# Weight sums on VectorE, and product reads as ScalarE copies with accumulating DMAs, in a two-layer streaming encoder

## The chip, the cores and the metric

The kernel runs on one core of one Trainium2 chip. A core has five engines, each with its own queue of instructions in a fixed order: TensorE (PE, with its weight loads as PEld), VectorE (DVE), ScalarE (ACT), GpSimd (POOL) and SyncE (SP). SP here does nothing but issue DMAs; POOL and ACT issue some as well. Data wait in SBUF, matmuls write to banks of PSUM, and DRAM holds inputs, outputs and spilled intermediates. Engines wait for each other and for DMAs by semaphores. The metric is the time of one execution on the device in microseconds, as the median of several runs.

## The reference

One inference step of a hybrid encoder of two layers, `DEPTH = 2`, for 1024 prompt tokens and 8 x 16 sample tokens, so nine tiles of 128 tokens with `D_MODEL = 1024` and `D_FF = 4096`. Layer 0 has sliding-window attention with its own keys and values, layer 1 attends over shared keys and values. What the change touches is the end of each layer:

```python
def mlp(x, g_norm, w_up, w_down):
    return jnp.square(jax.nn.relu(rmsnorm(x, g_norm) @ w_up)) @ w_down
...
        hp = hp + mlp(hp, g_mlp[layer], w_up[layer], w_down[layer])
        hs = hs + mlp(hs, g_mlp[layer], w_up[layer], w_down[layer])
```

The product with `w_down` (4096 x 1024) is added to the residual `hp` or `hs`. After layer 0 the sum is what layer 1 reads, after layer 1 it is the output. All data are float32.

## The kernel before, in words

A layer runs four stages: `attention`, `wo_phase` (output projection and norm), `mlp_up` and `mlp_down`. The residual of tile t lies in DRAM as `xd[t]`, 128 x 1024. Every float32 operand of a matmul is split in two parts, a rounded one (`hi`, cast on ACT, L128) and the remainder (`lo`, subtracted on DVE, L134), and a product is formed by three matmuls (`mm3`, L746 to L748).

The down projection does not multiply the plain blocks. `mlp_up` writes 20 forms of the hidden activations per half of `D_FF` to DRAM (`hd`, stores from POOL, L911). For each half, `mlp_down` multiplies each form with a combination of the eight raw weight blocks of that half (`W_FORMS`). There are 40 such products a layer. Each is three banks (one for each of three token tiles) of 12 matmuls of 128x512. The result of a product is then added to or taken from some of six outputs (`OUT_FORMS`): three parts of three tiles each (`PARTS`), by two halves of 512 columns. The products are put in chains (`CHAINS`): in a chain the same three banks go on accumulating, and only the difference between the output rows of a product and the next has to be read. So a bank is read between two products, and the next product of the chain may write to it only after that. The list `seq` holds the products in order with their reads; there are 41 reads a layer, each of three banks. Six banks give two chains room.

For product n the stage does this:

- `load_w` (SP): raw weight blocks not yet held, 1 MB each, into `r0` to `r10`; issued three products ahead (`AHEAD`).
- `load_h` (SP): the form, 768 KB, into `a0`, `a1` or `a2` in turn; it waits until PE is through with the product that used that buffer. `load` also ties these loads to each other in order.
- `add_w` (L1067): the sum or difference of two weight blocks, 128x2048, into `s0` or `s1`, on POOL, two products ahead. A combination of one block needs none.
- `split_w`: the split of the weights into `w0` or `w1`, and of the form in place, on ACT and DVE, one product ahead.
- the matmuls, and behind each bank the reads (L1119): DVE adds the bank into the tile of the residual.

The residual tiles `x0` to `x8` are loaded into SBUF at the start of the stage (`load_x`, at products 0, 1 and 3 of the order `X_AT`) and held there; a tile is stored after its last read. `DOWN_HOME` places all buffers of the stage, in an order that decides which of them share space with the last buffers of `mlp_up`, so that a load into them waits for the stores of `hd` from that space.

The text of the program is not the order on the engines: a planner orders each queue by priorities and its own estimates. A wait stops every later instruction of the same queue. In layer 0 `prep_bias`, called at product 20, prepares biases of layer 1 with DMAs of its own on SP.

## Time and profile before

| | us |
|---|---|
| median of 3 runs | 2477.91 (2471.18 to 2479.93) |
| the profiled execution | 2474.45 |
| its span, first to last instruction | 2472.3 |
| first and last start of `mlp_down` matmuls, layer 0 | 803.6 to 1196.8 |
| the same, layer 1 | 2079.1 to 2467.5 |
| granted TensorE clock, mean | 0.980 of full speed |

A row of instructions in the profile names the line, the engine, the operation, and the tiles as out<-in with buffer numbers left out: `a<-hd` is the load of a form, `s<-r,r` a weight sum, `w<-s` a split of a weight sum, `x<-x,ps_c` a read of a bank into the residual. Behind the count stand the busy time in us and the mean of one in ns, then the idle time before it and whoever ended it. Where a row stands for one tile, the three numbers are the least, the middle and the greatest duration in ns. A table of stretches gives the busy time of the engines and the number of instructions, then the granted clock, the mean busy share of the 16 DMA engines, and the rate in GB/s. Times in an order of events are us from the start of the span. Busy shares are averages over stages with different limits, so the stage concerned is read by itself.

### The profile page before, as it was taken

How to read it: one execution, taken by the hardware profiler on the slowest of the kernel's cores; microseconds unless marked ns; L12 is line 12 of the kernel's file. 1: busy time of each engine (PE TensorE's matmuls, PEld its weight loads, DVE VectorE, ACT ScalarE, POOL GpSimd, SP SyncE). 2: the span in 40 equal slices, each digit the busy share in tenths (PEclk: the TensorE clock that was granted, in tenths of full speed). 3: DMA queues.
4: the chain of work that ended last, by engine and by line, in shares of the span. 5: the costliest groups of instructions: out<-in, count | busy, mean ns of one | idle time of the engine just before them, and what ended most of it. 6: DMA issues, size and time to landing. Idle time of an engine off the chain costs nothing.

```text
span 2472.3 us, 33316 instructions
## 1 busy us (share of the span) xinstructions
PE 2311.3 (93%) x11429; PEld 1911.4 (77%) x11429; DVE 1848.3 (75%) x3128; ACT 1273.0 (51%) x2503; POOL 914.6 (37%) x956
## 2 busy tenths in 40 slices
PE   8998999999999789989999999998999998899989
PEld 6787877888888667767778788786888887677767
DVE  6788787665665888999577867877656566798995
ACT  3777674655555333333277766655555554233332
POOL 4434334122322554553233434344222223444650
PEclk9999999999999999999999999998999999899999
DMA  7445554243434643525544655543334336524523
GB/s 249 126 116 162 167 175 166 92 146 116 163 131 178 250 150 105 197 79 195 167 144 133 189 163 169 181 157 129 125 119 149 131 130 225 187 94 141 175 74 130
DMA packets 216376, 375.38 MB, mean 152 GB/s; under 512 B 51144, under 2 KB 125840, under 8 KB 216208
## 3 DMA queue, kind: packets, MB, share of 16 engines
q1 hardware_dynamic: 193136, 300.89, 37.8%
q0 software_dynamic: 21776, 67.65, 7.5%
q10 hardware_dynamic: 1296, 4.72, 0.5%
q8 instruction: 90, 1.47, 0.3%
q14 instruction: 78, 0.64, 0.1%
HBM read 241.23 MB, written 130.90 MB: 151 GB/s over the span
## 4 chain that ended last, share of the span: by engine, by line
PE 62%; DVE 18%; DMA 9%; issue 6%; ACT 3%; POOL 1%; SPq 0%; DVEq 0%; ACTq 0%; POOLq 0%
DVE a L134 5%; PE ps_x L746 5%; PE ps_x L748 5%; PE ps_x L747 5%; DVE w L134 3%; DMA a<-hd 3%; DVE x L1119 3%; PE ps_mm L217 3%; PE ps_c L746 3%; PE ps_c L747 3%; PE ps_c L748 3%; PE ps_mm L219 3%; PE ps_mm L218 3%; PE ps_y L748 2%; PE ps_y L747 2%
## 5 line engine op out<-in xcount | busy, mean ns | idle before, releaser
L746 PE MATMUL ps_c<-w,a 128*128 128x512 f32 x960 | 386.3, 402 | 62.2 <-DVE x L1119 54.7
L747 PE MATMUL ps_c<-w,a 128*128 128x512 f32 x960 | 385.0, 401 | 24.0 <-DVE w L134 23.9
L1067 POOL TENSOR_TENSOR s<-r,r 128x2048 f32<-128x2048 f32 x56 | 291.2, 5202 | 281.2 <-DVE w L134 160.4
L748 PE MATMUL ps_c<-w,a 128*128 128x512 f32 x960 | 383.1, 399 | 5.4 <-DVE a L134 5.4
L911 POOL DMA_DIRECT2D hd<-h x272 | 147.9, 544 | 582.4 <-ACT h L820 280.0
L134 DVE TENSOR_TENSOR a<-a 128x1536 fp32r<-128x1536 f32 x80 | 258.5, 3232 | 46.4 <-ACT a L128 46.4
L746 PEld LDWEIGHTS ps_c<-w,a 128*128 128x128 f32 x960 | 185.9, 194 | 113.7 <-DVE x L1119 36.9
L747 PEld LDWEIGHTS ps_c<-w,a 128*128 128x128 f32 x960 | 185.9, 194 | 67.6 <-DVE w L134 29.4
L128 ACT CAST a<-a 128x1536 fp32r<-128x1536 f32 x80 | 118.5, 1481 | 213.9 <-DMA a<-hd 213.8
L748 PEld LDWEIGHTS ps_c<-w,a 128*128 128x128 f32 x960 | 186.0, 194 | 47.1 <-DVE a L134 8.0
L128 ACT CAST w<-s 128x2048 fp32r<-128x2048 f32 x56 | 107.1, 1912 | 212.0 <-PE ps_c L748 177.9
L134 DVE TENSOR_TENSOR w<-s,w 128x2048 fp32r<-128x2048 f32 x56 | 176.3, 3150 | 21.8 <-ACT w L128 21.7
L1119 DVE TENSOR_TENSOR x<-x,ps_c 128x512 f32<-128x512 f32 x246 | 158.8, 676 | 35.7 <-PE ps_c L748 35.5
L217 PE MATMUL ps_mm<-w,hh 128*128 128x512 f32 x432 | 172.9, 401 | 6.5 <-POOL w L185 2.1
L219 PE MATMUL ps_mm<-w,hl 128*128 128x512 f32 x432 | 171.9, 399 | 1.2 <-DMA hl<-hTd 1.0
L218 PE MATMUL ps_mm<-w,hh 128*128 128x512 f32 x432 | 170.9, 396 | 1.4 <-DVE w L190 1.1
L746 PE MATMUL ps_x<-sx,w 128*128 128x512 f32 (+1 forms) x408 | 158.9, 390 | 3.4 <-ACT h L867 2.5
L747 PE MATMUL ps_x<-sx,w 128*128 128x512 f32 (+1 forms) x408 | 155.2, 380 | 0.0
L748 PE MATMUL ps_x<-sx,w 128*128 128x512 f32 (+1 forms) x408 | 155.2, 380 | 0.0
L128 ACT CAST w<-ru 128x512 fp32r<-128x512 f32 (+1 forms) x160 | 110.0, 708 | 84.4 <-PE ps_y L747 32.0
L134 DVE TENSOR_TENSOR ptl<-ps_tr,pth 128x512 fp32r<-128x512 f32 x180 | 122.4, 685 | 23.5 <-ACT pth L128 18.0
L134 DVE TENSOR_TENSOR w<-ru,w 128x512 fp32r<-128x512 f32 (+1 forms) x160 | 126.6, 793 | 15.2 <-ACT w L128 15.1
(280 smaller groups left out, 5972.6 us busy)
## 6 DMA issues: line engine op xcount, KB each, us to landing
a<-hd SPq DMA_DIRECT2D x80, 768.0 KB, 4.2
hd<-h POOLq DMA_DIRECT2D x272, 192.0 KB, 2.5
ru<-in_w_up SPq DMA_DIRECT2D x64, 512.0 KB, 3.8
r<-in_w_down SPq DMA_DIRECT2D x32, 1024.0 KB, 8.7
x<-xd SPq DMA_DIRECT2D x41, 512.0 KB, 6.4
o<-oTd SPq DMA_DIRECT2D x52, 256.0 KB, 4.4
xd<-xo SPq DMA_DIRECT2D x18, 512.0 KB, 2.8
xo<-xd SPq DMA_DIRECT2D x18, 512.0 KB, 3.7
```

The costliest lines, as they stand in the source:

```text
L128: a = nc.scalar.copy(hi, src)
L134: return a, e.tensor_tensor(lo, src, hi.bitcast(F32), ALU.subtract)
L217: nc.tensor.matmul(ps, a, w[:, 0, k, :], start=(k == 0), stop=False)
L218: nc.tensor.matmul(ps, a, w[:, 1, k, :], start=False, stop=False)
L219: self.lp = nc.tensor.matmul(ps, b, w[:, 0, k, :], start=False, stop=(k == KC - 1))
L746: a = mm(ps, ah, bh, start=first, stop=False, skip_group_check=True)
L747: mm(ps, ah, bl, start=False, stop=False, skip_group_check=True)
L748: return a, mm(ps, al, bh, start=False, stop=last, skip_group_check=True)
L911: return lambda p, z: self.nc.gpsimd.dma_start(self.hd[c // 4][:, p, c % 4], z)
L1067: nc.gpsimd.tensor_tensor(src[n], x, y, ALU.add if plus else ALU.subtract)
L1119: tt(x, x, banks[i], ALU.add if v > 0 else ALU.subtract)
```

## The change

It has four parts, all in or for `mlp_down`.

- The weight sums are made by DVE instead of POOL.
- Of the 41 reads a layer, only the last read of each of the six outputs is still a DVE addition. For it, SP loads the three half tiles (128x512, 256 KB) of the residual from DRAM into `f` buffers (six, in turn) at that product, DVE adds the bank, and SP stores the half tile to its destination.
- The other 35 reads become ACT copies of the three banks into an `o` buffer (128 x 3 x 512; four, in turn), with the sign as the scale, and one accumulating DMA of the buffer into the residual in DRAM, issued by POOL.
- The `x` tiles and their loads at the start are gone. `o` and `f` buffers take their places in `DOWN_HOME`. In DRAM the residual is now three tensors `xp`, one for each part, and `xd[t]` is a view of one.

```diff
-                s=([P, 4, 512], F32), x=([P, D], F32),
+                s=([P, 4, 512], F32), o=([P, 3, 512], F32), f=([P, 512], F32),
...
-                nc.gpsimd.tensor_tensor(src[n], x, y, ALU.add if plus else ALU.subtract)
+                tt(src[n], x, y, ALU.add if plus else ALU.subtract)
...
-            def load_x(i):
-                for t in PARTS[i]:
-                    load(xs[t], self.xd[t])
...
                 a, w = aa.pop(n), ws.pop(n)
+                ends, adds = {}, {}
+                for o, v in reads:
+                    part, h = divmod(o, 2)
+                    if left[o] == n:
+                        for i in range(3):
+                            ends[o, i] = take(f"f{nf % 6}")
+                            nf += 1
+                            nc.sync.dma_start(ends[o, i], self.xd[PARTS[part][i]][:, N[h]])
+                    else:
+                        adds[o] = take(f"o{no % 4}")
+                        no += 1
                 for i in range(3):
...
                     for o, v in reads:
-                        x = xs[PARTS[o // 2][i]][:, N[o % 2]]
-                        tt(x, x, banks[i], ALU.add if v > 0 else ALU.subtract)
-                    for part in {o // 2 for o, _ in reads}:
-                        if last[part] == n:
-                            t = PARTS[part][i]
-                            nc.sync.dma_start(out(t), xs[t])
+                        part, h = divmod(o, 2)
+                        if o in adds:
+                            nc.scalar.activation(adds[o][:, i], banks[i], AF.Copy, scale=float(v))
+                        else:
+                            x, t = ends[o, i], PARTS[part][i]
+                            tt(x, x, banks[i], ALU.add if v > 0 else ALU.subtract)
+                            nc.sync.dma_start(out(t)[:, N[h]], x)
+                for o, z in adds.items():
+                    part, h = divmod(o, 2)
+                    dst = self.xp[part][:, :, N[h]].rearrange("t p n -> p t n")
+                    nc.gpsimd.dma_start(dst, z, accum_op=ALU.add)
...
-            self.xd = [dram([P, D], f"xd{t}") for t in range(NTILE)]
+            self.xp = [dram([3, P, D], f"xp{i}") for i in range(3)]
+            self.xd = {t: self.xp[i][n] for i in range(3) for n, t in enumerate(PARTS[i])}
...
 DOWN_HOME = (
-    "s0", "s1", "r0", "r1", "r2", "r3", "x5", "x6", "x7", "bias", "r4", "r5", "+384", "x2", "x3", "x0", "+640",
-    "a0", "x4", "x1", "x8", "r6", "a1", "a2", "w0", "w1", "r7", "r8", "r9", "r10",
+    "s0", "s1", "r0", "r1", "r2", "r3", "o2", "o3", "bias", "r4", "r5", "+384", "o0", "f0", "f1", "f2", "+640",
+    "a0", "f3", "f4", "o1", "f5", "r6", "a1", "a2", "w0", "w1", "r7", "r8", "r9", "r10",
 )
```

In the built program the other stages keep their order on every engine, apart from the first steps of layer 1's attention, which the planner weaves into the end of layer 0's `mlp_down` a little differently. POOL has only the 35 accumulating DMAs between the last store of `hd` and the next stage. An accumulating DMA waits for the copies it sends and for the accumulating DMA before it that went to the same output; an ACT copy waits for the accumulating DMA that last used its buffer.

More of the change, by code (lines that the diff above doesn't have):

```diff
@@ L978, in mlp_down @@
                 a=([P, 2, 4, 3 * P], F32R), w=([P, 2, 4, 512], F32R), r=([P, 4, 512], F32),
-                s=([P, 4, 512], F32), x=([P, D], F32),
+                s=([P, 4, 512], F32), o=([P, 3, 512], F32), f=([P, 512], F32),
             )
-            homes, slots, xs = {}, {}, {}
+            homes, slots = {}, {}
             def fresh(tag):
@@ L1000, in mlp_down @@
                         slots[t] = fresh(t)
-            for t in range(NTILE):
-                xs[t] = slots.pop(f"x{t}")
             N = [slice(0, 512), slice(512, 1024)]
@@ L1023, in mlp_down @@
                     left[i] = n
-            last = {i // 2: max(left[i], left[i ^ 1]) for i in left}
             aa, ws = {}, {}
@@ L1077, in mlp_down @@
             banks = None
+            nf = no = 0
             def early(n):
                 return self.tc.high_priority(EARLY[n]) if n < len(EARLY) else nullcontext()
-            def load_x(i):
-                for t in PARTS[i]:
-                    load(xs[t], self.xd[t])
             for n in range(AHEAD):
@@ L1089, in mlp_down @@
                     load_h(n)
-                if n in X_AT:
-                    load_x(X_AT[n])
             add_w(0)
@@ L1099, in mlp_down @@
                     load_w(n + AHEAD)
-                if n + AHEAD in X_AT:
-                    load_x(X_AT[n + AHEAD])
                 split_w(n + 1)
@@ L1782 @@
 AHEAD = 3
-X_AT = {0: 2, 1: 1, 3: 0}
 WO_ORDER = [[0, 4, 1, 5, 2, 6, 7, 3, ST], [0, 4, 1, 5, 6, 2, 7, 3, ST]]
```

## The prediction

> **What bounds the kernel now.** I read the page first, then the down-projection stage (`mlp_down`) by the stretches in which its products run, since the change touches only this stage and the first steps after it. Two rows of the page, and the product matmuls (`ps_c`) over four stretches (columns: stretch, its length, busy time and count of PE, PEld and DVE, granted clock, DMA share, GB/s):

> ```profile
> span 2472.3 us, 33316 instructions
> PE 2311.3 (93%) x11429; PEld 1911.4 (77%) x11429; DVE 1848.3 (75%) x3128; ACT 1273.0 (51%) x2503; POOL 914.6 (37%) x956
> ...
> 803.00:900.00 97.00, 77.83 (x315) 61.70 (x316) 19.41 (x30) 0.93 0.67 233
> 900.00:1197.00 297.00, 266.06 (x1127) 213.21 (x1125) 59.35 (x92) 0.98 0.40 136
> 2079.00:2180.00 101.00, 81.03 (x313) 64.22 (x314) 19.95 (x31) 0.86 0.51 184
> 2180.00:2468.00 288.00, 265.71 (x1129) 214.42 (x1127) 58.73 (x92) 0.98 0.36 123
> ```

> PE is 93% busy over the span, but not here. A stretch in which it never waits gives its pace; a stretch of the up-projection beside it shows that PE can hold that pace at full clock:

> ```profile
> 980.00:1020.00 40.00, 40.00 (x178) 33.14 (x177) 34.60 (x26) 16.82 (x10) 13.00 (x4) 1.00 0.57 197
> 1920.00:1960.00 40.00, 40.00 (x201) 34.01 (x200) 24.76 (x40) 21.84 (x37) 10.84 (x20) 1.00 0.40 137
> ```

> 178 matmuls in 40 us are 0.225 us each; a product is 36, so 8.1 us, and a layer's 1440 are 324 us. Layer 0 takes 97 + 297 = 394 us and layer 1 101 + 288 = 389: 70 and 65 us lost. At 0.225 us the counts split that into a start (97 - 315 x 0.225 = 26 us; 31 us) and the rest (44; 35). The waits of PE in each layer's stage (total us, times, longest) name who is late most, and the order of time shows why (a step of DVE, POOL and ACT from layer 1):

> ```profile
> PE ps_c L746 <- DVE x L1119: 29.8, 13, 6.0
> PE ps_c L746 <- DVE x L1119: 24.9, 12, 5.9
> ```

> ```profile
> 2193.79 1.27 DVE L1119 TENSOR_TENSOR x<-x,ps_c 128x512 f32<-128x512 f32 x2
> 2194.99 2.28 DVE L134 TENSOR_TENSOR w<-s,w 128x2048 fp32r<-128x2048 f32 x1
> 2197.19 0.67 DVE L1119 TENSOR_TENSOR x<-x,ps_c 128x512 f32<-128x512 f32 x1
> 2197.79 5.79 DVE L134 TENSOR_TENSOR a<-a 128x1536 fp32r<-128x1536 f32 x1
> ...
> 2197.34 4.62 POOL L1067 TENSOR_TENSOR s<-r,r 128x2048 f32<-128x2048 f32 x1 [5.09 <-DVE w L134]
> ...
> 2200.34 1.91 ACT L128 CAST w<-s 128x2048 fp32r<-128x2048 f32 x1 [3.78 <-PE ps_c L748]
> 2204.43 1.49 ACT L128 CAST a<-a 128x1536 fp32r<-128x1536 f32 x1 [2.18 <-DMA a<-hd]
> ```

> The split of `a` starts 0.45 us after POOL's sum and ends (2203.58) 1.6 us after POOL's end (2201.96): DVE stood still while POOL ran. The smallest times show what each costs alone:

> ```profile
> L134 DVE TENSOR_TENSOR a<-a x80: 1739/1759/6099, 795.5 to 2457.4; 128x1536 fp32r<-128x1536 f32 x80
> L134 DVE TENSOR_TENSOR w<-s,w x28: 2273/2279/6705, 826.8 to 1143.6; 128x2048 fp32r<-128x2048 f32 x28
> L1067 POOL TENSOR_TENSOR s<-r,r x56: 4537/4620/11987, 800.7 to 2394.6; 128x2048 f32<-128x2048 f32 x56
> L1119 DVE TENSOR_TENSOR x<-x,ps_c x246: 669/675/689, 816.3 to 2468.0; 128x512 f32<-128x512 f32 x123
> ```

> So DVE's step is 1.27 + 2.28 + 0.67 + 5.79, overlaps off, about 9.7 us against PE's 8.1, and the bank reads (x) behind the stopped split hold PE. The bound of the stage is DVE, and 4 us of its step are POOL's.

> **The change, part by part.**

> *Weight sums to DVE.* Two f32 inputs of 128x2048 are the shape of the `w` split: 2.28 us in place of 4.62 on POOL and of the stop on DVE. 64 sums in two layers are 32 a layer. DVE per layer then: 40 x 1.74 + 40 x 2.28 + 32 x 2.28 + 18 x 0.67 = 246 us, 6.2 a product, against 336 now (row below). Four products of the last third form two sums: 1.74 + 3 x 2.28 = 8.6 us, 0.5 over PE; 2 us a layer.

> *Reads to ACT.* Of 41 reads a layer, 6 are an output's last and stay on DVE (18 adds); 35 become 105 ACT copies of a bank. Prices of this part and the next, by line, by the stage of layer 1, and by its DMA issues (KB each, us to landing):

> ```profile
> L867 ACT COPY h<-ps_x x34: 373/572/589, 445.6 to 2058.7; 128x512 f32<-128x512 f32 x30, 128x256 f32<-128x256 f32 x4
> L911 POOL DMA_DIRECT2D hd<-h x272: 542/542/603, 460.1 to 2101.9; - x136
> 2079.00:2468.00 389.00, 346.86 (x1442) 278.63 (x1440) 335.94 (x217) 132.63 (x82) 173.69 (x46) 0.95 0.40 139
> a<-hd SPq DMA_DIRECT2D x37, 768.0 KB, 4.1
> r<-in_w_down SPq DMA_DIRECT2D x13, 1024.0 KB, 8.4
> hd<-h POOLq DMA_DIRECT2D x11, 192.0 KB, 2.4
> ```

> ACT per product: 1.9 + 1.5 + 105/40 x 0.58 = 4.9 us, and 6.9 where two outputs are read: below 8.1. But ACT now has three duties in one order: weight cast, copy of bank 0, `a` cast, copies of banks 1 and 2. The `a` cast waits for its load, which PE's end of a product releases and which lands 4.1 us later; a copy behind it must be done when the next product comes back to the bank. Bank 1 is wanted 8.1 + 2.7 = 10.8 us after the release, so the load may take about 10.8 - 1.5 - 1.2 = 8 us before PE waits. That is 4 us of slack, so at today's landing the copies cost PE nothing.

> *Accumulating DMAs.* 35 a layer, 786,432 bytes each, all issued by POOL, which has nothing else here; by the `hd` stores an issue is 0.54 us for 128 rows, so at most 1.6 us for 384 rows, against one each 8 us. No row shows an accumulating transfer. Cheap end: a load of that size, 4.1 us. Costly end: three such transfers one after the other (read addend, read residual, write), 12.3 us. I take two passes, because the residual is read and written back once, as one load and one store. The stage now moves 139 GB/s at a share of 0.40, so 347 GB/s when full; two passes of 27.5 MB are 158 us of full use a layer. With today's 0.40 x 389 = 156 us, that is 314 of some 335 us. Residual loads and stores keep their bytes. So the DMA engines are nearly full, and in products 19 to 30 (12 products, 97 us) more than full: 15 accumulates (2 x 11.8 MB), 12 `a` loads (9.4 MB) and 8 weight loads (8.4 MB) need 41.4 MB / 347 GB/s = 119 us. Four copy buffers let the accumulates lag some 15 us, so of the 22 us over I charge 10, and 5 for the crowded first products: 15 us a layer.

> [...]

> *Buffers and waits.* A copy buffer is free again when its accumulate, four earlier, has landed. Where two pairs follow (products 6 and 7, 19 and 20, 28 and 29), the gap from issue to reuse is 8.1 + 2.7 - 0.6 = 10.2 us; elsewhere 18 or more. At 4.1 plus one more pass and some sharing (7 to 9 us) that holds. Behind the waiting copy stand the `a` and weight casts, and behind those PE. The 18 last adds of a layer wait for a 256 KB load on SP, asked for at their product's place; the accumulate before lies two to six products back, so nothing. The outputs' stores (halves) stand on SP ahead of `a` loads, and wait for DVE adds; 1 us each at some places, 3 us a layer.

> *No x tiles held.* At the start SP stood behind the last group of x loads, whose space the up-projection frees last:

> ```profile
> 2076.59 32.50 SPq L1031 DMA_DIRECT2D x<-xd  x3
> 2109.20 0.36 SPq L1031 DMA_DIRECT2D a<-hd  x1
> 2109.62 0.43 SPq L1031 DMA_DIRECT2D r<-in_w_down  x1
> ...
> 2106.10 0.54 POOL L911 DMA_DIRECT2D hd<-ht  x1 [2.45 <-DVE ht L968]
> ...
> 2115.48 1.47 ACT L128 CAST a<-a 128x1536 fp32r<-128x1536 f32 x1 [17.94 <-DMA a<-hd]
> ...
> 2086.92 4.97 DVE L943 TENSOR_TENSOR ht<-h 128x384 f32<-128x384 f32 x1
> ```

> `a` and the weights follow only at 2109. Now they are asked for when a product ends, from about 2087. What is late next: the copies of product 1 go to buffers in that same space, and wait for the last `hd` store. DVE reaches that store earlier by the eight bank reads (5 us) and the stop in L943 (4.4), later by two sums (4.6): about 2101 instead of 2106, landing 2.4 us on. Product 2 wants its bank at 2079 + 16 = 2095, so 8 us stay, and 2 for slow matmuls after a stop: 10 a layer. Won: 26 + 31 - 20 = 37 us.

> *Sum.* Rest of the stages 44 + 35 = 79, starts 37: 116 us off. Back: transfers 30, SP 6, DVE 4: 40. 116 - 40 = 76. The profiled execution took 2474.45 us (span 2472.3), 3.5 under the median 2477.91; against the median, 2402.

> **The rivals.** *Transfers hidden altogether.* If an accumulate costs the one pass of a load, products 19 to 30 need 29.6 MB, 85 us of 97: 2478 - 106 = 2372. For it: share 0.36 now. This is the forecast's low side.

> *Casts behind waits.* Sharing takes the `a` load past 8 us, ACT stands at its cast, and the copies behind it hold PE. For it: a weight load that shares with an `a` load today takes 8.4 us. Against: 4 us of slack. If 24 products lose 1 us each, a layer loses 24: 2402 + 48 = 2450.

> *Transfers become the bound (slower).* The place is POOL's queue and the 16 DMA engines; 35 accumulates must pass while products 0 to 33 run. With 10 us start and six products (49 us) outside, today's 392 us a layer (the mean of 394 and 389) are reached when one takes (392 - 59) / 35 = 9.5 us on average: that decides. At three passes with full overlap, 238 + 156 = 394 us plus the start's 10 are 404 a layer, +12: 2502. At 12.3 us each with none, 35 x 12.3 + 59 = 490, +98 a layer: 2674. For it: no row shows that accumulates overlap, and adds into the same output must follow one another. Against: loads do overlap and reach 347 GB/s. [...]

> *Nothing:* gain and cost cancel, 2478.

> **How the numbers follow.** Forecast with the hidden case, 2360 to 2440: 0.50; casts behind waits, 2440 to 2465: 0.12; nothing: 0.06; transfer-bound up to 2530: 0.17; beyond: 0.15. A measurement tells 0.5% (12 us) from no change. Faster 0.62, same 0.06, slower 0.32. The range 2360 to 2530 leaves out the heavy transfer case and 3 in 100 below; the forecast's own range is 2360 to 2440.

> **What would show it.** Right: `a` splits at 1.74 us throughout, sums near 2.28, waits of PE on bank reads gone from the list, 8.1 us a product, accumulates landing in 6 to 9 us, stages near 355 us. Wrong: ACT copies waiting for accumulates, `a` loads landing beyond 8 us, the DMA share near 1 over products 19 to 30, POOL's issues far above 1.6 us.

## The result and the profile after

The changed kernel takes 2507.5 us in the median (2499.74 to 2510.81), the kernel before, run beside it, 2474.55 us (2468.32 to 2479.93): a ratio of 1.013, with a 95% interval of 1.0093 to 1.0166. It is 33 us slower, where 76 us faster was forecast. The profiled execution is the fastest of its runs, 2499.74 us; its span is 25.6 us longer than that of before. First a row of its page, then the product matmuls (`ps_c`) in four stretches (columns as in the prediction, with ACT behind DVE): the first 100 us of each layer's stage, and the rest of it.

```profile
PE 2317.5 (93%) x11429; PEld 1921.3 (77%) x11429; DVE 1668.7 (67%) x2982; ACT 1376.2 (55%) x2713; POOL 664.5 (27%) x962
```

```profile
804.00:904.00 100.00, 79.54 (x316) 63.73 (x317) 0.00 (x0) 17.45 (x32) 0.88 0.89 241
904.00:1208.00 304.00, 271.88 (x1124) 220.12 (x1123) 11.49 (x17) 41.63 (x74) 0.94 0.87 219
2094.00:2194.00 100.00, 81.06 (x336) 66.33 (x337) 0.00 (x0) 18.50 (x33) 0.90 0.80 207
2194.00:2494.00 300.00, 264.83 (x1106) 214.43 (x1104) 11.57 (x18) 40.58 (x72) 0.94 0.84 206
```

At 0.225 us a matmul the stretches lose 29, 51, 24 and 51 us; before, in the prediction's stretches, it was 26, 43, 31 and 34 by the same working (the prediction has 44 and 35). The stages grew by some 10 us each (394 to 404, 389 to 399), which is 20 of the 26; the others lie outside. The gain at the start is as good as absent, and the rest of each stage is worse. The DMA share, 0.36 to 0.40 in the long stretches before, is 0.84 to 0.87. POOL and DVE have both become lighter (914.6 to 664.5 us and 1848.3 to 1668.7) and neither shows in the end time.

The part of the change on DVE did what it was to do (form split and weight sum, ns least/middle/greatest):

```profile
L134 DVE TENSOR_TENSOR a<-a x80: 1748/1759/2190, 792.8 to 2484.0; 128x1536 fp32r<-128x1536 f32 x80
L1063 DVE TENSOR_TENSOR s<-r,r x56: 2280/2292/2295, 794.5 to 2410.2; 128x2048 f32<-128x2048 f32 x56
```

The greatest split is 2.2 us, where it was 6.1. And over products 9 to 20 of layer 1, of which all but the last two have one accumulate or none, PE runs without a gap at full clock (all engines, PE, PEld, DVE, ACT, POOL):

```profile
2194.00:2294.00 100.00, 100.00 (x443) 82.84 (x442) 69.75 (x34) 57.91 (x59) 15.19 (x12) 1.00 0.96 222
2314.00:2420.00 106.00, 78.36 (x312) 62.45 (x312) 58.54 (x30) 42.81 (x45) 15.20 (x12) 0.90 0.84 190
```

443 matmuls in 100 us are the ideal pace, and the DMA share there is 0.96, so a high share by itself does not stop PE. The second row, products of the second half of `D_FF` with their pairs of accumulates, shows where the time goes: 312 x 0.225 = 70 us of work in 106. Both rows have 12 accumulates in some 100 us: POOL's queue goes no faster where more stand in line. Who is late there is a wait that the kernel before did not have (by layer, total us, times, longest):

```profile
PE ps_c L746 <- ACT o L1120: 27.5, 6, 8.3
PE ps_c L746 <- ACT o L1120: 39.2, 6, 11.8
```

It is 66.7 us, in place of the 54.7 us of waits for DVE's bank reads (29.8 + 24.9). ACT in turn waits for accumulating DMAs (`xp<-o`), 121.3 us in 26 waits, which the prediction had named as a sign of being wrong. The copies of products 22, 23 and 24 of layer 1 do so, with the casts of the next product behind them:

```profile
2304.27 0.60 ACT L1120 ACTIVATE o<-ps_c 128x512 f32<-128x512 f32 x1 [4.18 <-DMA xp<-o]
...
2315.72 1.08 ACT L1120 ACTIVATE o<-ps_c 128x512 f32<-128x512 f32 x2 [6.70 <-DMA xp<-o]
2316.69 1.47 ACT L128 CAST a<-a 128x1536 fp32r<-128x1536 f32 x1
...
2328.98 0.60 ACT L1120 ACTIVATE o<-ps_c 128x512 f32<-128x512 f32 x1 [8.52 <-DMA xp<-o]
```

Why those land late is on POOL's queue. The accumulates (KB each, median us to landing), POOL's order of time in layer 1 (the last four rows are the accumulates of products 19 and 20), and the part of POOL's idle time ahead of all 70 that has no releaser (us, times):

```profile
xp<-o POOLq DMA_DIRECT2D x70, 768.0 KB, 7.8
```

```profile
2172.35 1.27 POOL L1128 DMA_DIRECT2D xp<-o  x1 [10.69 <-DMA xp<-o]
2180.05 1.26 POOL L1128 DMA_DIRECT2D xp<-o  x1 [6.43 <-issue]
2187.76 1.26 POOL L1128 DMA_DIRECT2D xp<-o  x1 [6.44 <-DMA xp<-o]
...
2284.36 1.27 POOL L1128 DMA_DIRECT2D xp<-o  x1 [13.26 <-ACT o L1120]
2292.12 1.26 POOL L1128 DMA_DIRECT2D xp<-o  x1 [6.48 <-issue]
2304.51 1.26 POOL L1128 DMA_DIRECT2D xp<-o  x1 [11.12 <-issue]
2315.95 1.27 POOL L1128 DMA_DIRECT2D xp<-o  x1 [10.18 <-issue]
```

```profile
  issue: 287.8, 34
```

The first three issues stand 7.70 us apart, the duration of one accumulate, although by the order of the products each goes to another output than the one before it (4, 3, 5). 34 of the 70 were held by nothing that the profile names ("issue"), 287.8 us in all. No two of the 70 are issued less than 7.28 us apart, so the accumulates do not overlap. The copies of products 19 and 20 were all done by 2291, but the fourth accumulate begins only at 2315.95; the ACT waits above end where the second, third and fourth of them have landed.

### The profile page after: what moved, and what is told of

It reads as the page before. It is cut to its first block, busy times and chain, and to the rows that moved or that the text cites. A ratio compares the mean times of both kernels' runs of the same rounds, so it can differ in the third digit from the quotient of the medians.

```text
span 2497.9 us, 33524 instructions
## 1 busy us (share of the span) xinstructions
PE 2317.5 (93%) x11429; PEld 1921.3 (77%) x11429; DVE 1668.7 (67%) x2982; ACT 1376.2 (55%) x2713; POOL 664.5 (27%) x962
## 3 DMA queue, kind: packets, MB, share of 16 engines
q8 instruction: 90, 1.47, 0.2%
## 4 chain that ended last, share of the span: by engine, by line
PE 40%; DMA 11%; issue 7%; DVE 4%; ACT 3%; POOL 1%; SPq 0%; POOLq 0%; ACTq 0%; DVEq 0%
PE ps_c L748 4%; PE ps_c L746 4%; PE ps_c L747 4%; DMA xp<-o 4%; PE ps_x L746 2%; PE ps_x L748 2%; PE ps_x L747 2%; PE ps_mm L217 2%; PE ps_mm L219 2%; PE ps_mm L218 2%; DMA a<-hd 2%; PE ps_tr L324 1%; DMA xp<-f 1%; PE ps_y L748 1%; PE ps_y L747 1%
## 5 line engine op out<-in xcount | busy, mean ns | idle before, releaser
L746 PE MATMUL ps_c<-w,a 128*128 128x512 f32 x960 | 391.5, 408 | 97.8 <-ACT o L1120 66.7
L747 PE MATMUL ps_c<-w,a 128*128 128x512 f32 x960 | 388.4, 405 | 5.5 <-DVE w L134 5.5
L748 PE MATMUL ps_c<-w,a 128*128 128x512 f32 x960 | 388.2, 404 | 2.9 <-DVE a L134 2.9
L911 POOL DMA_DIRECT2D hd<-h x272 | 147.2, 541 | 587.0 <-ACT h L820 288.1
L746 PEld LDWEIGHTS ps_c<-w,a 128*128 128x128 f32 x960 | 189.7, 198 | 146.8 <-ACT o L1120 71.8
L134 DVE TENSOR_TENSOR a<-a 128x1536 fp32r<-128x1536 f32 x80 | 141.0, 1762 | 210.4 <-ACT a L128 210.4
L1128 POOL DMA_DIRECT2D xp<-o x70 | 88.8, 1268 | 578.2 <-issue 287.8
L128 ACT CAST a<-a 128x1536 fp32r<-128x1536 f32 x80 | 118.3, 1479 | 202.7 <-DMA a<-hd 202.7
L1120 ACT ACTIVATE o<-ps_c 128x512 f32<-128x512 f32 x210 | 118.2, 598 | 195.5 <-DMA xp<-o 121.3
L747 PEld LDWEIGHTS ps_c<-w,a 128*128 128x128 f32 x960 | 189.4, 197 | 46.5 <-DVE w L134 6.6
L748 PEld LDWEIGHTS ps_c<-w,a 128*128 128x128 f32 x960 | 188.6, 196 | 45.7 <-DVE a L134 5.2
L134 DVE TENSOR_TENSOR w<-s,w 128x2048 fp32r<-128x2048 f32 x56 | 128.1, 2288 | 49.7 <-ACT w L128 47.6
L746 PE MATMUL ps_x<-sx,w 128*128 128x512 f32 (+1 forms) x408 | 157.9, 387 | 3.7 <-ACT h L867 2.7
L128 ACT CAST w<-ru 128x512 fp32r<-128x512 f32 (+1 forms) x160 | 110.0, 708 | 84.0 <-PE ps_y L747 32.0
L748 PE MATMUL ps_x<-sx,w 128*128 128x512 f32 (+1 forms) x408 | 154.2, 378 | 0.0
L1063 DVE TENSOR_TENSOR s<-r,r 128x2048 f32<-128x2048 f32 x56 | 128.1, 2290 | 26.6 <-DMA r<-in_w_down 25.6
L134 DVE TENSOR_TENSOR ptl<-ps_tr,pth 128x512 fp32r<-128x512 f32 x180 | 122.3, 685 | 23.6 <-ACT pth L128 17.5
L134 DVE TENSOR_TENSOR w<-ru,w 128x512 fp32r<-128x512 f32 (+1 forms) x160 | 126.7, 794 | 14.8 <-ACT w L128 14.7
## 6 DMA issues: line engine op xcount, KB each, us to landing
a<-hd SPq DMA_DIRECT2D x80, 768.0 KB, 5.8
xp<-o POOLq DMA_DIRECT2D x70, 768.0 KB, 7.8
hd<-h POOLq DMA_DIRECT2D x272, 192.0 KB, 2.5
r<-in_w_down SPq DMA_DIRECT2D x32, 1024.0 KB, 10.3
```

The lines of the kernel that those rows point to most:

```text
L128: a = nc.scalar.copy(hi, src)
L134: return a, e.tensor_tensor(lo, src, hi.bitcast(F32), ALU.subtract)
L746: a = mm(ps, ah, bh, start=first, stop=False, skip_group_check=True)
L747: mm(ps, ah, bl, start=False, stop=False, skip_group_check=True)
L748: return a, mm(ps, al, bh, start=False, stop=last, skip_group_check=True)
L911: return lambda p, z: self.nc.gpsimd.dma_start(self.hd[c // 4][:, p, c % 4], z)
```

## The experiments

Three theories stood at the start. Q: POOL's queue has room for only one DMA of this size, so each begins after the one before has landed. F: the 16 DMA engines are full, and the queue does not matter. S: f loads that wait on SP for late accumulates hold the loads of the forms. Times are medians, and ratios go to the kernel before on the same chip.

**One part alone: the sums (`e1_sums_only`).** The kernel before, with

```diff
-                nc.gpsimd.tensor_tensor(src[n], x, y, ALU.add if plus else ALU.subtract)
+                tt(src[n], x, y, ALU.add if plus else ALU.subtract)
```

> The kernel before with one part of the change alone: the weight sums on DVE; reads stay DVE additions into x tiles. The part is worth what POOL's sum cost DVE: an a split of 5.79 us becomes 1.74, a sum of 2.28 comes in. DVE per layer by rows: 40 x 1.74 + 40 x 2.28 + 32 x 2.28 + 41 x 3 x 0.675 = 317 us, against PE's 324. Theory A (the sums were right in the prediction, the accumulating DMAs are what spoilt it): the waits in mid-stage fall from 79 us to some 30, the starts (57 us) stay: about 2425, between 2405 and 2445. Theory B (DVE at 98% of PE's time is a bound as before, and the sums bring nothing without the reads moved): 2465 to 2490.

2398.1 us, ratio 0.9696 (0.9675 to 0.9716). The four stretches (PE, PEld, DVE):

```profile
800.00:900.00 100.00, 83.29 (x337) 65.71 (x338) 20.95 (x32) 0.93 0.67 233
900.00:1163.00 263.00, 254.26 (x1105) 207.31 (x1103) 60.34 (x91) 0.99 0.45 153
2038.00:2138.00 100.00, 89.09 (x368) 71.65 (x369) 22.99 (x35) 0.95 0.54 194
2138.00:2390.00 252.00, 245.20 (x1073) 200.47 (x1071) 58.32 (x88) 1.00 0.41 138
```

Losses are 24 and 17 us at the start and 14 and 11 in the rest. One line of the change brings 76 us; the time lies 7 us below theory A's range, and theory B falls. It is chance that 76 us is also what was forecast for the whole change, since the forecast added it up from other terms as well. DVE at 317 us of work beside PE's 324 a layer (both from the expectation) is not a bound that hurts here, where the longest form split is 2.14 us and not 6.10. The remainder of the change costs 2507.5 - 2398.1 = 109 us on top of it.

**The other part alone: the reads (`e6_reads_only`).** The changed kernel with that line put back to POOL.

> The changed kernel with the weight sums back on POOL: the part of the change that moves the reads, alone. If the parts add up (the sums are worth -76 us alone), the reads are worth +109 and this gives about 2583. If POOL's queue decides (an accumulating DMA holds POOL until the one before has landed, 7.7 us, and the sums of 4.62 us stand in the same queue): 35 x 7.7 + 32 x 4.62 = 417 us of POOL a layer and some 15 at the start, 40 over before's 391: about 2555. If moving the reads off DVE relieves it (1.74 + 2.28 + 4.05 us of stop are 8.1 a product, PE's own pace): under 2470.

2563.2 us, ratio 1.0388 (1.0343 to 1.0432), nearest to 2555, the sum by POOL's queue. POOL near the end of layer 1:

```profile
2403.57 1.27 POOL L1128 DMA_DIRECT2D xp<-o  x1 [6.22 <-issue]
2404.40 9.44 POOL L1063 TENSOR_TENSOR s<-r,r 128x2048 f32<-128x2048 f32 x2
2413.59 1.51 POOL L1128 DMA_DIRECT2D xp<-o  x1
```

Two sums stand behind an accumulate that waited 6.22 us, and the next accumulate behind them. The expectation by simple addition, 2583, is only 20 us away, and the longest run (2582.26) reaches it, so the time alone does not part these two; the rows show the queue.

**More room for POOL's DMAs (`e3_room`).** More of the SBUF that the program sets aside for POOL's DMAs (for their descriptors, by the expectation), paid for from gaps in the layout:

```diff
-            self.pad(top, "edge", 104, "right")
...
-    "s0", "s1", "r0", "r1", "r2", "r3", "o2", "o3", "bias", "r4", "r5", "+384", "o0", "f0", "f1", "f2", "+640",
+    "s0", "s1", "r0", "r1", "r2", "r3", "o2", "o3", "bias", "r4", "r5", "+160", "o0", "f0", "f1", "f2", "+640",
...
-    nc = bacc.Bacc("TRN2", target_bir_lowering=False, num_devices=1, dynamic_dma_scratch_size=1024)
+    nc = bacc.Bacc("TRN2", target_bir_lowering=False, num_devices=1, dynamic_dma_scratch_size=1920)
```

> The changed kernel with more SBUF for the descriptors of POOL's DMAs: 1920 bytes a partition in place of 1024, taken from gaps between buffers. Nothing else differs. Theory Q: two accumulating DMAs can stand in the queue at once, issues no longer spaced by the landing (7.7 us) but by 1.3 us where the copies are there, and the pairs of reads at products 6 and 7, 19 and 20 hold up nobody: stages 20 us shorter each, about 2465. Theory F: DMA share is the bound, landings just become longer (10 us or more with two in flight): 2500 to 2515.

2450.1 us, ratio 0.9904 (0.9873 to 0.9935): 57 us less than the changed kernel. POOL's order at the pairs, the unexplained part of POOL's idle time ahead of the accumulates, and the stretches of `ps_c`:

```profile
2319.38 2.55 POOL L1128 DMA_DIRECT2D xp<-o  x2 [17.98 <-ACT o L1120]
```

```profile
  issue: 42.7, 10
```

```profile
807.00:907.00 100.00, 81.79 (x335) 66.28 (x336) 0.00 (x0) 18.09 (x33) 0.93 0.99 275
907.00:1191.00 284.00, 261.85 (x1107) 212.88 (x1105) 11.53 (x18) 40.78 (x72) 0.96 0.86 228
2074.00:2174.00 100.00, 90.87 (x387) 74.53 (x388) 0.00 (x0) 20.33 (x37) 0.95 0.95 255
2174.00:2440.00 266.00, 248.29 (x1055) 201.83 (x1053) 11.37 (x17) 38.13 (x68) 0.97 0.84 220
```

Two accumulates are issued without a pause (x2, 2.55 us), the unexplained idle time falls from 287.8 to 42.7 us, POOL mostly waits for the copies, and the copies wait 1.5 us in all for accumulates, in place of 121.3. Theory Q holds. F has one part right: with two in flight an accumulate lands after 10.7 us in the median. The edit also moves some buffers; no run takes that by itself, but 39 of the 54 us that the stretches win lie behind the first 100 us of each stage.

But the queue is not all: the stretches still lose 25, 35, 13 and 29 us, 101 together, and the DMA share is 0.84 to 0.99. PE still waits 39.6 us for copies: 17.3 us in two waits at the starts, where the copies wait for the last `hd` store, and 22.3 us in seven where ACT stood at a cast whose form came late, with the copies behind it:

```profile
2355.81 1.47 ACT L128 CAST a<-a 128x1536 fp32r<-128x1536 f32 x1 [9.58 <-DMA a<-hd]
2357.19 1.08 ACT L1120 ACTIVATE o<-ps_c 128x512 f32<-128x512 f32 x2
```

A third place in the queue was not tried.

**Plain stores (`e4_plain`).** The changed kernel with

```diff
-                    nc.gpsimd.dma_start(dst, z, accum_op=ALU.add)
+                    nc.gpsimd.dma_start(dst, z)
```

where `dst` lies in another DRAM tensor `xq`.

> The changed kernel with the accumulating DMA replaced by a plain store of the copy buffer to another DRAM tensor: the addition of 35 of 41 reads a layer is left out. Same issues by POOL, same 768 KB, one pass in place of two. Theory Q: still one at a time, but the landing falls to some 4 to 5 us, so 35 of them take 175 us and lag nowhere: waits on ACT copies gone, stages near 365 us, about 2430. Theory F gives about the same here, since the share falls too; the two differ in the spacing of issues, which Q puts at the landing and F at the copies (1.3 us where two are ready). If the copies' order on ACT or the SP queue were the cause, the time would stay near 2500.

2385.0 us, ratio 0.9653 (0.9619 to 0.9687). The four stretches, and a row of POOL:

```profile
809.00:909.00 100.00, 90.77 (x385) 73.42 (x386) 0.00 (x0) 20.60 (x37) 0.98 0.83 293
909.00:1160.00 251.00, 243.53 (x1056) 199.45 (x1055) 11.58 (x17) 38.81 (x68) 0.99 0.67 237
2042.00:2142.00 100.00, 95.65 (x415) 78.86 (x416) 0.00 (x0) 21.83 (x39) 0.98 0.74 266
2142.00:2379.00 237.00, 233.46 (x1027) 192.10 (x1025) 11.44 (x17) 37.38 (x66) 1.00 0.65 230
```

```profile
2272.41 1.49 POOL L1128 DMA_DIRECT2D xq<-o  x2 [17.91 <-ACT o L1120]
```

Losses of 13, 13, 7 and 6 us, and 2385.0 where both theories said about 2430. Everything else in the changed kernel works: the copies on ACT, four copy buffers, the loads; PE's waits for copies fall to 9.6 us. It also shows what moving the reads wins where nothing is accumulated: 13 us beyond the sums alone (2398.1). So the 109 us are 57 for the queue's room and 65 for the accumulating, less these 13. A plain store of the same size takes POOL 0.75 us in place of 1.26, and two stand in the queue with the old room, which Q, as it was put, had not said ("still one at a time").

**Smaller pieces (`e2_split3`, `e9_room_thirds`).** The first splits each accumulate of the changed kernel by token tile; the second has the larger room as well and issues each third behind its own copy.

```diff
-                    nc.gpsimd.dma_start(dst, z, accum_op=ALU.add)
+                    for i in range(3):
+                        nc.gpsimd.dma_start(self.xp[part][i][:, N[h]], z[:, i], accum_op=ALU.add)
```

> The changed kernel, each accumulating DMA of 768 KB given as three of 256 KB (one for each token tile), same buffers, same bytes, same places. Theory Q (POOL's queue has room for one DMA of 384 rows, so one starts only when the one before has landed, each taking 7.7 us): three small ones fit at once, transfers follow each other without the gap between landing and next issue; spacing of 768 KB falls from 7.7 to about 5 us, the waits of PE on the ACT copies (66.7 us) mostly go, about 2460. Theory F (the 16 DMA engines are full, share 0.92 to 1.03 where adds follow each other): the same spacing of 7.7 us and the same time, 2500 to 2515. Theory L (every DMA on that queue waits for the one before, whatever its size): three landings of 3 us or more each, spacing 9 to 12 us, 2560 or more.

> The kernel with more SBUF for POOL's descriptors, and each accumulating DMA as three of 256 KB, each issued right behind the ACT copy of its bank: the finest use of the queue tried. With 768 KB each and the same room 2450.1 us, with plain stores 2385.0. Theory F (what is left of those 65 us is the doubled pass on the 16 DMA engines, 4.5 us of all 16 for each 768 KB against 2.0): 2435 to 2455, spacing no matter. Theory Q (the queue's few places are still the limit): transfers start up to 5 us earlier and overlap freely, 2400 to 2420. Theory I (three issues at 0.86 us and three completions in place of one cost more): 2460 or more.

2463.1 us (ratio 0.9962, 0.9943 to 0.9981) and 2479.1 us (1.0012, 0.9997 to 1.0026). The first fits Q, though POOL still stands 110.5 us without a releaser. In the second, POOL's unexplained idle time is 8.6 us, so the queue holds nobody; yet it is 29 us slower than the larger pieces with the same room, as theory I had it. POOL's issues (105 x 0.865 us a layer) are no bound. The loads tell more, here the weight loads of `e9_room_thirds` and then of `e3_room`:

```profile
r<-in_w_down SPq DMA_DIRECT2D x32, 1024.0 KB, 13.5
```

```profile
r<-in_w_down SPq DMA_DIRECT2D x32, 1024.0 KB, 9.3
```

With more small accumulates in flight, the loads that PE waits for land later (a form in 6.5 us, 5.1 in `e3_room`), and PE's waits for the split of weights grow from 10.9 to 29.0 us. That this is the reason for the 29 us is argued from these rows, and no run takes it by itself.

**Twice the plain store (`e11_plain_twice`).** `e4_plain` with a second store of the same buffer to a third tensor `xr`, so that the data pass twice without any adding.

> The changed kernel with each accumulating DMA replaced by two plain stores of the copy buffer, to two other DRAM tensors: the addition of 35 of 41 reads a layer is left out, the data pass over the DMA engines twice (an accumulate by our rows 4.5 us of all 16 engines, a plain store 2.0). With one store 2385.0, with accumulating DMAs and room for two 2450.1. Theory F (the doubled pass is what the accumulate costs once the queue is not the limit): 2430 to 2460. Theory M (the cost lies in the accumulating itself, a read of the residual that must come back before the write): the stores stay hidden like the single ones, 2385 to 2400.

2428.0 us, ratio 0.9799 (0.9772 to 0.9826): 43 of the 65 us between single stores (2385.0) and accumulates with room (2450.1). It ends 2 us under theory F's range and far above M's. POOL's DMA queue (packets, MB, share of the 16 engines) of before, after, `e4_plain` and `e11_plain_twice`; in `e3_room` the share is 20.5%:

```profile
q0 software_dynamic: 21776, 67.65, 7.5%
```

```profile
q0 software_dynamic: 49776, 122.71, 21.1%
```

```profile
q0 software_dynamic: 36336, 122.71, 13.5%
```

```profile
q0 software_dynamic: 50896, 177.76, 19.0%
```

Times the spans (2472.3, 2497.9, 2383.1, 2431.5, and 2444.1 for `e3_room`), less the 185 us of before, by 70: an accumulate occupies all 16 engines for 4.9 us, with more room 4.5; a plain store for 1.95, and two for 3.95. So two plain passes cost most of what the accumulate costs without the queue's limit. One thing stays open: this run has the old room, and POOL stands 70.6 us without a releaser ahead of the first of its two stores alone; PE waits 17.3 us for copies (9.6 in `e4_plain`), but what the queue has of the 43 us is not known. The last 22 us of the 65 are not split; the next runs put some 5 of them on the f loads.

**f loads that wait for no accumulate (`e7_f_input`, `e8_room_f_input`).** In the changed kernel, and in the one with more room:

```diff
-                            nc.sync.dma_start(ends[o, i], self.xd[PARTS[part][i]][:, N[h]])
+                            nc.sync.dma_start(ends[o, i], self.xp_in[i * P : (i + 1) * P, N[h]])
```

> The changed kernel, with the f loads taken from a prompt input of the same size instead of the residual: the last read of each output is added to the wrong rows, so the accumulated residual is left out of what is stored. The loads keep their place on SP and their bytes but wait for no accumulating DMA. Theory S (f loads that wait on SP hold the loads of the forms behind them): the waits of PE on f adds (14.9 us) and on casts of late forms (15.4) go, and with them the tail: about 2470. Theory N (what holds PE is ACT at its copies, because the queue takes 7.7 us per accumulate; f loads wait only beside that): 2495 to 2510.

> The kernel with more SBUF for POOL's descriptors (2450.1 us), with the f loads taken from the prompt input as in the run before this one. It asks what the 65 us between that kernel and the one with plain stores (2385.0) are. Theory F (two passes of data: DMA share 0.84 to 0.98 against 0.65 to 0.83 with plain stores): no change, 2440 to 2455. Theory S (the f loads on SP still wait for accumulating DMAs that land 10.7 us after issue): 2405 to 2425.

2477.3 us (ratio 1.0017, 0.9989 to 1.0046) and 2444.6 us (0.9893, 0.9866 to 0.9921). In the changed kernel the waits of the f loads cost 30 us, nearer to S than to N; once the accumulates no longer lag, 5.5 us, as F had it. The rows of the changed kernel show the mechanism (SP, then ACT):

```profile
2405.80 1.27 SPq L1103 DMA_DIRECT2D f<-xp  x3
2407.18 0.36 SPq L1027 DMA_DIRECT2D a<-hd  x1
```

```profile
2416.97 1.47 ACT L128 CAST a<-a 128x1536 fp32r<-128x1536 f32 x1 [15.42 <-DMA a<-hd]
```

A form is asked for only behind the f loads of the product, these wait for the last accumulate, and ACT stands 15 us at its cast. So S is a second effect of Q: the lag of POOL's queue comes to PE by ACT's copies and by SP's loads.

**The start by itself (`e5_late_x`, `e10_before_late_x`).** The third group of x loads asked for later, with the sums on DVE and without:

```diff
-X_AT = {0: 2, 1: 1, 3: 0}
+X_AT = {0: 2, 1: 1, 7: 0}
```

> The kernel before with the weight sums on DVE (2398.1 us) and one more edit: the third group of x loads, at which SP stands 31.7 and 31.5 us at the start of the stage, is asked for with the loads of product 7 and not of product 3; its first read is at product 8. The prediction said of the start that SP stands behind these loads and that PE's loss there (26 and 31 us before) goes with them, 37 of 57 us won. If that reading holds, the first 100 us of each stage lose 5 to 10 us in place of 24 and 18: 2365 to 2380. If the start is limited by the hd stores and the first splits themselves, no change: 2393 to 2400.

> The kernel before, only the third group of x loads moved from product 3 to product 7. With the sums on DVE the same edit gave 2398.1 to 2382.1, 16 us. If the start's stall is a loss of its own, 12 to 30 us here too: 2445 to 2463. If DVE, the bound while POOL makes the sums, only waits elsewhere instead: within 6 us of 2474.5.

2382.1 us (ratio 0.9633, 0.96 to 0.9665) and 2464.5 us (0.9954, 0.9938 to 0.997). With the sums on DVE, this is the fastest kernel of all, 125 us under the changed one, though 2 us above the range that was expected. SP at the start of layer 1 of `e1_sums_only` and of `e5_late_x`, then the first stretches of the latter:

```profile
2035.51 31.46 SPq L1031 DMA_DIRECT2D x<-xd  x3
```

```profile
2071.95 1.69 SPq L1031 DMA_DIRECT2D x<-xd  x3
```

```profile
800.00:900.00 100.00, 91.44 (x389) 73.59 (x390) 23.21 (x36) 0.98 0.71 241
...
2034.00:2134.00 100.00, 95.67 (x418) 78.31 (x419) 25.45 (x39) 1.00 0.61 210
```

SP no longer stands, and the starts lose 12 and 6 us in place of 24 and 17, as the reading of the start had it, a little short of the expected 5 to 10 in layer 0. Without the sums on DVE the same edit brings 10 us, between its two expectations, so it is not settled how much of the start DVE takes back there.

## Why the prediction was wrong, step by step

- *DVE bounds the stage, and POOL's sum stops it.* Right. `e1_sums_only` takes this cause away alone and wins 76 us; the mid-stage losses of 43 and 34 us become 14 and 11. A form split took 5.79 us beside POOL's sum of 4.62, and 1.76 in the median; in the changed kernel, with no sums on POOL, the longest is 2.19 us beside 70 accumulate issues, and with the sums back on POOL (`e6_reads_only`) it is 10.64. What the two engines share there was not shown.
- *Sums at 2.28 us, ACT copies at 0.58.* Right: 2.29 and 0.60.
- *The single accumulate.* Right in each of its prices: issue 1.26 us (at most 1.6 was said), landing 7.8 us (6 to 9), and 4.9 us of all engines (4.5 in `e3_room`), near the two passes as taken (786,432 bytes twice at the prediction's 347 GB/s are 4.5, an estimate). A plain store took 1.95 us of all engines (`e4_plain`), so an accumulate is 2.3 to 2.5 of it.
- *"At 4.1 plus one more pass and some sharing (7 to 9 us) that holds."* This step failed. It compares the gap of 10.2 us with the landing of one accumulate, as if each could start when its copies are done. POOL's queue has room for one here, so a pair that follows a pair stands behind it: the four accumulates of products 19 and 20 start 7.8, 12.4 and 11.4 us apart. The first buffer, the one with the gap of 10.2 us, was free in time; for the other three ACT stands 4.2, 6.7 and 8.5 us. ACT stands 121.3 us in all, and PE waits 66.7 us for its copies; room for a second accumulate alone wins 57 us. The rival had named "no row shows that accumulates overlap" and set against it that loads do; loads go by SP's queue. On POOL's queue the `hd` stores of 192 KB do follow each other faster than they land (three in 1.75 us, landing after 2.5), but no row had DMAs of 768 KB there.
- *The rival "transfers become the bound".* This is what came true, at POOL's queue first, and the place was named. Its 0.17 was too little. That its 2502 lies 5 us from the measured 2507.5 is luck: it counts three passes with full overlap, and the runs show about two (4.5 to 4.9 us of all engines, plain stores 1.95) and, at the old room, no overlap.
- *"15 us a layer" for full DMA engines.* Mis-sized, even with the queue's limit lifted: `e3_room` loses 101 us in its stretches and `e4_plain` 39, so 31 a layer. Of the 65 us between the two kernels, 43 come back with a second plain pass.
- *The rival "casts behind waits".* Its mechanism is what `e3_room` shows once the queue has room: ACT stands at a cast whose form is late, and PE waits for the copies behind it, 22 us in both layers together where the rival charged 48. That `e3_room` took 2450.1 us and the rival said 2450 is luck.
- *f loads on SP, "so nothing".* Wrong as a consequence: 30 us by `e7_f_input`, since the accumulate "two to six products back" had not landed. Where the queue keeps up it is 5.5 us, nearly the nothing that was said.
- *The start, 57 to 20 us.* The mechanism was right: with plain stores the starts lose 13 + 7 = 20 us, the very number, and SP alone gives 24 + 17 to 12 + 6 in `e5_late_x`. In the changed kernel they lose 29 + 24 and with more room 25 + 13, so in layer 1 the queue takes about as much as the accumulating, and in layer 0 it is mostly the accumulating.
- *The sum.* Without the accumulate's two costs the rest comes out close: `e4_plain`, which leaves the adding out, has 39 us of loss where the prediction, less its 30 us for transfers, had 30, and 2385.0 against its 2402 and the 2372 of "transfers hidden altogether".

## What to carry to other kernels

Ask of a DMA not only how long it takes but how many of its kind can be under way on its queue: look for issues spaced by one landing, with idle time that no semaphore explains (7.70 us and 287.8 us here). Where a change has two halves, price each by itself: here one line was worth 76 us and the rest cost 109. Before data are moved from an engine to the DMA engines, count the passes (4.9 us of the 16 engines for an accumulate here, 1.95 for a plain store) against their share in the stage, not in the span, and look at the loads which the new transfers will delay (a form landed after 4.2 us before and 5.8 after).
